# A batched A·Bᵀ on one Trainium2 core: one more batch of loads ahead of the first store, and a small early write into the output

## The chip, the cores and the metric

The kernel runs on one core of one Trainium2 chip. The metric is the device time of one execution, in microseconds (us). The kernel before took 126.73 us (median of 4; 126.66 to 126.77); over all the rounds in which it ran again beside the experiments, single runs of it went from 126.33 to 127.32, so one run alone says little about differences under 0.5 us.

## The reference

```python
def setup_inputs():
    batch, m, k, n = 16, 512, 512, 512
    return {"a": np.random.randn(batch, m, k).astype(np.float32),
            "b": np.random.randn(batch, n, k).astype(np.float32)}

def reference(a, b):
    return np.matmul(a, b.transpose(0, 2, 1)).astype(np.float32)
```

Sixteen independent products. Each batch reads 1 MB of a and 1 MB of b and writes 1 MB of out (1,048,576 bytes each): 48 transfers in all.

## The kernel before

Per batch it loads a and b, converts both to bf16 on VectorE, turns (transposes) them on TensorE, multiplies there, copies the result out of PSUM on ScalarE, and stores it. All 48 transfers are issued by SyncE, in program order:

```python
    AHEAD = 5
    apool = ctx.enter_context(tc.tile_pool(name="a_pool", bufs=6))
    bpool = ctx.enter_context(tc.tile_pool(name="b_pool", bufs=6))
    ...
    opool = ctx.enter_context(tc.tile_pool(name="o_pool", bufs=5))
    ...
    def load(i):
        a_sb = apool.tile([P, J, K], f32, tag="a")
        b_sb = bpool.tile([P, J, K], f32, tag="b")
        nc.sync.dma_start(a_sb[:], a[i].rearrange("(p j) k -> p j k", j=J))
        nc.sync.dma_start(b_sb[:], b[i].rearrange("(p j) k -> p j k", j=J))
        return a_sb, b_sb
    ...
    def store(i, o_sb):
        nc.sync.dma_start(out[i].rearrange("(p j) n -> p j n", j=J), o_sb[:])

    loaded = {}
    with tc.manual_schedule():
        for i in range(min(AHEAD, batch)):
            loaded[i] = load(i)
        for i in range(batch):
            a_sb, b_sb = loaded.pop(i)
            a_h = halve(a_sb, "a")                  # VectorE: f32 -> bf16
            b_h = halve(b_sb, "b")
            aT = turn(a_h, "a", nc.scalar.copy)     # TensorE, then a copy out of PSUM
            bT = turn(b_h, "b", nc.vector.tensor_copy)
            o_sb = multiply(aT, bT)                 # TensorE, then four ScalarE copies into o_sb
            store(i, o_sb)
            if i + AHEAD < batch:
                loaded[i + AHEAD] = load(i + AHEAD)
```

So ten loads precede store 0 in the queue; after that the order is store, load, load.

## Time and profile before

| What | Value | Where it is read |
|---|---|---|
| time, span | 126.73 us, 124.9 us | runs, page |
| TensorE, ScalarE, VectorE busy | 74%, 55%, 47% | page, part 1 |
| the SyncE queue's packets, as a share of 16 engines' span | 96.9% | page, part 3 |
| bytes over the span | 403 GB/s | page, part 3 |
| rate in the steady stretch, 40 to 80 us | 425 GB/s | stretches |
| rate from 25.5 to 28.0 us | 288 GB/s | stretches |

The transfer engines are the bound, so the way to read this profile is to look for places where they move less than 425 GB/s, and then to ask which of the sixteen ends last. A stretch in which they are busy (share near 1.00) and yet move clearly less is called a hole below; the turn is the place in the queue where the first store follows a run of loads. The trace keeps sixteen landing times for each transfer (768 for the 48), one for each engine's part; the transfer has landed at the last of them. The times don't carry the engine's name, so I sort them; an engine that lies a microsecond or more behind the other fifteen can still be followed from transfer to transfer. I use the landings below as a **lateness**: the landing time of an engine's part of transfer k, less 5.0 + 2.4526 x (k - 1) us. The slope is what the slowest engine of this kernel needed per transfer from transfer 13 to 48, (124.07 - 38.23)/35; the offset is arbitrary. A stall raises an engine's lateness, and it stays raised: in the kernel before the fastest engine stands at 0.91 us from transfer 10 and still at 0.95 at transfer 47. The line stands at 120.27 us for transfer 48, so a last landing 3.80 us late is one at 124.07.

### The profile page before, as it was taken

Reading aid. Unit: us, or ns where it says so; the run is one execution under the profiler, and the core shown is the slowest. Engines: PE = TensorE matmul, PEld = TensorE weight load, DVE = VectorE, ACT = ScalarE, POOL = GpSimd, SP = SyncE. Lnnn points to the kernel's source line nnn. Section 1 sums busy time; section 2 is a strip of 40 time slices with the busy share of each in tenths; the row PEclk is TensorE's granted clock in tenths of the full one; section 3 lists DMA queues with packets and bytes.
Section 4 is the critical chain, followed back from the end, with each engine's and each line's share of the span. In section 5 each row is a group of like instructions: output and inputs, shape, how many; then the busy total and the mean of one; then the engine's idle time right before and its main releaser. Section 6 shows DMA issues by size and latency. Waiting matters only on the chain.

```text
span 124.9 us, 1885 instructions
## 1 busy us (share of the span) xinstructions
PE 92.2 (74%) x754; PEld 55.9 (45%) x768; DVE 59.2 (47%) x64; ACT 68.3 (55%) x97; POOL 0.7 (1%) x6
## 2 busy tenths in 40 slices
PE   0069989898989878949586794958769495886900
PEld 0056465655656445534544453444445344454300
DVE  0156555647373554374446537444653645456000
ACT  4041576777767683755738275582826649173610
POOL 2000000000000000000000000000000000000000
PEclk9999999999999999999999999999999999999995
DMA  3999999999999999999999999999999999999982
GB/s 89 420 433 430 430 425 420 412 317 420 425 422 428 430 425 425 420 433 422 430 422 422 422 433 417 428 425 422 430 428 425 422 422 422 430 430 420 415 352 113
DMA packets 6922, 50.46 MB, mean 404 GB/s; under 512 B 769, under 2 KB 769, under 8 KB 769
## 3 DMA queue, kind: packets, MB, share of 16 engines
q1 hardware_dynamic: 6912, 50.33, 96.9%
q8 instruction: 6, 0.10, 0.3%
q14 instruction: 4, 0.02, 0.0%
HBM read 33.55 MB, written 16.78 MB: 403 GB/s over the span
## 4 chain that ended last, share of the span: by engine, by line
DMA 80%; DVE 6%; PE 5%; SPq 3%; issue 1%; ACT 0%; DVEq 0%
DMA b_sb<-in_b_dram 80%; DVE half L52 4%; PE ps L75 3%; PE tp L62 2%; DVE turned L67 2%; SPq L46 1%; SPq L47 1%; ACT o_sb L80 0%; DVEq L52 0%
## 5 line engine op out<-in xcount | busy, mean ns | idle before, releaser
L75 PE MATMUL ps<-turned 128*128 128x512 bf16 x242 | 59.8, 382 | 6.1 <-DVE turned L67 5.5
L80 ACT COPY o_sb<-ps 128x512 f32<-128x512 f32 x64 | 37.5, 586 | 44.0 <-PE ps L75 40.8
L62 PE MATMUL tp<-ident,half 128*128 128x128 bf16 x512 | 34.8, 225 | 20.1 <-DVE half L52 20.0
L62 PEld LDWEIGHTS <-half 128*128 128x128 bf16 x512 | 31.3, 101 | 25.6 <-DVE half L52 23.7
L75 PEld LDWEIGHTS <-turned 128*128 128x128 bf16 x256 | 25.1, 98 | 36.6 <-issue 10.7
L67 ACT COPY turned<-tp 128x1024 bf16<-128x1024 bf16 x32 | 30.8, 1016 | 6.0 <-PE tp L62 6.0
L52 DVE CAST half<-a_sb 128x2048 bf16<-128x2048 f32 x16 | 19.6, 1224 | 22.0 <-DMA a_sb<-in_a_dram 22.0
L67 DVE COPY turned<-tp 128x1024 bf16<-128x1024 bf16 x32 | 20.7, 686 | 19.3 <-PE tp L62 19.3
L52 DVE CAST half<-b_sb 128x2048 bf16<-128x2048 f32 x16 | 19.6, 1226 | 14.8 <-DMA b_sb<-in_b_dram 14.8
L67 ACT ACT_TABLE_LOAD x1 | 1.3, 1283 | 0.7 <-PEq L117 0.7
masks.py:199 POOL TENSOR_SCALAR_AFFINE_SELECT ident<-ident 128x128 bf16<-128x128 bf16 x1 | 0.3, 292 | 0.1
masks.py:197 POOL MEMSET ident<- 128x128 bf16 x1 | 0.2, 204 | 0.3 <-POOLq L117 0.3
L117 POOL MEMSET const-bfloat16-1.0<- 128x1 bf16 x1 | 0.1, 101 | 0.0
L117 POOL MEMSET const-uint8-127<- 128x1 uint8 x1 | 0.1, 101 | 0.0
L117 POOL MEMSET const-float32-0.0<- 128x1 f32 x1 | 0.1, 98 | 0.2 <-issue 0.2
L117 POOL MEMSET const-float32-1.0<- 128x1 f32 x1 | 0.1, 98 | 0.0
## 6 DMA issues: line engine op xcount, KB each, us to landing
a_sb<-in_a_dram SPq DMA_DIRECT2D x16, 1024.0 KB, 19.6
b_sb<-in_b_dram SPq DMA_DIRECT2D x16, 1024.0 KB, 19.6
out_dram<-o_sb SPq DMA_DIRECT2D x16, 1024.0 KB, 19.6
```

Source lines behind the costliest of these rows:

```text
L46: nc.sync.dma_start(a_sb[:], a[i].rearrange("(p j) k -> p j k", j=J))
L47: nc.sync.dma_start(b_sb[:], b[i].rearrange("(p j) k -> p j k", j=J))
L52: nc.vector.tensor_copy(out=half[:], in_=src[:])
L62: nc.tensor.transpose(tp[:, h, j * P:(j + 1) * P], half[:, j, (ko + h) * P:(ko + h + 1) * P], ident[:],)
L67: copy(out=turned[:, ko:ko + 2, :], in_=tp[:])
L75: nc.tensor.matmul(ps[:], aT[:, ko, j * P:(j + 1) * P], bT[:, ko, :], start=(ko == 0), stop=(ko == KO - 1),)
L80: nc.scalar.copy(out=o_sb[:, j, :].rearrange("m (p j) -> m p j", j=J), in_=ps[:].rearrange("m (j p) -> m p j", j=J),)
L117: nc = _bacc.Bacc("TRN2", target_bir_lowering=False, num_devices=1)
```

## The change

The intent, as far as the code tells it: the rate falls when the first store comes up, so a first write into out is made early, beside the start-up of the loads, and the first store is moved back by one batch. Two more load buffers are paid for by one output buffer.

```diff
-    AHEAD = 5
+    AHEAD = 6
-    apool = ctx.enter_context(tc.tile_pool(name="a_pool", bufs=6))
-    bpool = ctx.enter_context(tc.tile_pool(name="b_pool", bufs=6))
+    apool = ctx.enter_context(tc.tile_pool(name="a_pool", bufs=7))
+    bpool = ctx.enter_context(tc.tile_pool(name="b_pool", bufs=7))
-    opool = ctx.enter_context(tc.tile_pool(name="o_pool", bufs=5))
+    opool = ctx.enter_context(tc.tile_pool(name="o_pool", bufs=4))
...
+    zero = const.tile([P, P], f32)
+    nc.vector.memset(zero, 0.0)
     with tc.manual_schedule():
+        nc.scalar.dma_start(out[0].rearrange("(p j) n -> p j n", j=J)[:, 0, :P], zero[:])
         for i in range(min(AHEAD, batch)):
             loaded[i] = load(i)
```

## The prediction

> **What bounds the kernel now.** I read the page's rows of the span first, then stretches of the span, then the issue queue, then the end of the chain of waits. The page has the transfers near their ceiling in all but three places:
>
> ```profile
> DMA  3999999999999999999999999999999999999982
> GB/s 89 420 433 430 430 425 420 412 317 420 425 422 428 430 425 425 420 433 422 430 422 422 422 433 417 428 425 422 430 428 425 422 422 422 430 430 420 415 352 113
> HBM read 33.55 MB, written 16.78 MB: 403 GB/s over the span
> ```
>
> A slice is 124.9/40 = 3.12 us. No engine is above 74% (PE) over the span, so compute only matters where a transfer waits for it. The weak slices are the first (89, start-up), the ninth (317, at 25.0 to 28.1 us) and the last two (352, 113). The stretches, cut at the edges of these holes (columns: stretch, length, busy time and count on PE, weight loads, VectorE, ScalarE, GpSimd, then clock, DMA share, GB/s):
>
> ```profile
> 3.12:24.50 21.38, 16.12 (x130) 10.64 (x133) 11.27 (x13) 10.29 (x14) 0.00 (x0) 1.00 1.01 424
> 25.50:28.00 2.50, 2.50 (x23) 1.49 (x21) 0.99 (x1) 1.68 (x4) 0.00 (x0) 1.00 1.00 288
> 40.00:80.00 40.00, 31.45 (x264) 18.80 (x267) 20.00 (x22) 23.31 (x34) 0.00 (x0) 1.00 1.01 425
> 118.40:120.10 1.70, 0.06 (x1) 0.00 (x0) 0.00 (x0) 0.58 (x1) 0.00 (x0) 1.00 0.70 294
> ```
>
> From 25.5 to 28.0 us the DMA share stays 1.00 while the rate falls to 288: the engines have work, but it goes slowly. The loss is 2.50 x (1 - 288/425) = 0.81 us averaged over the sixteen engines. It is the only such place in mid-run. Ten loads of 1 MB precede store 0 in the one SyncE queue; the tenth is moving then, and store 0 is next. All later stores pass at 425. So something is paid once, around the first turn from loads to stores.
>
> The issue queue shows it from the side of the slowest engine (start, duration):
>
> ```profile
> 5.64 0.33 SPq L46 DMA_DIRECT2D a_sb<-in_a_dram  x1
> 8.08 0.33 SPq L47 DMA_DIRECT2D b_sb<-in_b_dram  x1
> 16.30 0.35 SPq L87 DMA_DIRECT2D out_dram<-o_sb  x1
> ...
> 24.54 0.33 SPq L47 DMA_DIRECT2D b_sb<-in_b_dram  x1
> 28.10 0.34 SPq L87 DMA_DIRECT2D out_dram<-o_sb  x1
> 30.91 0.33 SPq L46 DMA_DIRECT2D a_sb<-in_a_dram  x1
> 33.37 0.33 SPq L47 DMA_DIRECT2D b_sb<-in_b_dram  x1
> ```
>
> The trace has eight semaphores for transfers, so a transfer is issued when the one eight before it has landed on its slowest engine. The issues at 5.64, 24.54 and 30.91 therefore time the landings of transfers 1, 8 and 10. In the steady part issues are (92.33 - 53.04)/16 = 2.456 us apart: the time of 1 MB. From 5.64, seven more should end at 22.83; the eighth ends at 24.5, 1.65 late. From there two more should end at 29.4; the tenth ends at 30.9, 1.5 late. The landings' records agree: the first of the sixteen engines finishes transfer 8 at 22.49 and the last at 24.48, and an instruction fetch of 16 KB sits at 22.1 (1.0 us) on one engine. That engine stays some 2.4 to 2.8 us behind the fastest to the end.
>
> Budget: 5.64 + 47 x 2.456 = 121.07; the last landing is at 124.07; the 3.0 between are the fetch and restart on the slow engine (about 1.6) and the first-store hole (about 1.45 on that engine, 0.8 on average). The span ends 0.8 later, and the time is 1.8 over the span.
>
> The end of the chain (start, us, what):
>
> ```profile
> 92.33 19.57 DMA b_sb<-in_b_dram
> 111.90 0.03 issue
> ...
> 118.49 0.58 ACT o_sb L80
> ```
>
> The last load lands at 111.90, its result is ready at 119.07, the last store goes out at 119.1. The page ends its chain in compute, but this is not what binds: fast engines drain at about 118.4 and idle (the 294 above), while the slow engine lands store 14 at 121.65 and store 15 at 124.07, 2.42 later, which is one transfer without a pause. The end belongs to the slow engine's unbroken stream.
>
> **What the Trainium skill says.** "HBM Reference", Specifications: a core streaming alone reaches about 425 GB/s, bounded by its 16 engines. The trace agrees: 424 and 425. "DMA: Bandwidth & Descriptors", Issuing engines are not separate DMA queues: what ScalarE issues runs on the same sixteen engines and interleaves. So the zeros bring no bandwidth. No second issuing queue is in this trace, but the instruction fetches, a foreign queue too, do displace packets: at 71.37 an 8 KB fetch took 0.31 us and the packet after it 0.86 instead of 0.31. The same page, Back-pressure in remote DMA: stalled writes stall an engine's other queues too. That is said for remote transfers; nothing in this trace shows whether it holds for a first write to out. It is the main argument against the change.
>
> **The change part by part.**
>
> *AHEAD 5 to 6, pools of 7.* Two loads change places with store 0: it becomes transfer 13 of 48 and starts some 4.9 us later. No bytes are added. Store 0's data is ready at 16.3; as transfer 13 it would get its semaphore when transfer 5 lands, at 15.5, so SyncE is not blocked longer than now, and eight transfers (19.6 us of work) stay queued. The hole would merely move from 26 to about 31 us. At the end the last load is transfer 42 in place of 43, so compute of batch 15 gets 2.456 us more lead. This end doesn't bind, so it is worth 0.
>
> *o_pool 5 to 4.* In steady state store i is transfer 13+3i, and load b of batch i+4 is transfer 3i+9. The first eviction of batch i+4 comes 115.90 - 111.90 = 4.0 us after that landing, but now needs store i, four transfers later, 9.8 us. So ScalarE will wait some 5.8 us for each buffer: a new wait. It paces compute at one batch per three transfers (7.37 us), against some 5.9 that a batch needs (first evictions at 24.90, 30.80, 36.70), so it holds the rhythm and starves no transfer: a store is due 12 transfers after the one whose buffer it took. In the tail, batch 14 evicts when store 10 lands (transfer 43), four evictions of 0.58 back to back are 2.4, the two turned copies of batch 15 are 1.93, its first eviction comes some 0.6 later and its last ends 3.2 after that: 8.1 us after the landing of transfer 43. Transfer 47 lands 9.8 after it, and a store needs about 1 us from issue to its first packet. Slack is 0.7 against 1.5 now: thin, worth 0.
>
> *The zeros.* One memset of 128x128 on VectorE (GpSimd's of that form took 0.20 us) and one issue on ScalarE (0.4 as SyncE's first ones), both before ScalarE's first copy at 8.00: off the path. On the engines 64 KB are 8 pieces of 512 B each, 4 KB in all: 0.15 us of bytes at 26.6 GB/s an engine. If they fall into the first 1.1 us, in which the first load packets wait for their data, they cost about 0.2; in a running stream about 0.15 + 0.55 for the restart, as after the fetch: 0.7. I take 0.4, an estimate. Store 0 must wait for the zeros to land, long past by then.
>
> If the hole is the price of the first write to out, and if it is paid beside the start-up, the slow engine gains 1.4: 126.73 - 1.4 + 0.4 = 125.7.
>
> **Rivals.**
> 1. *The stall moves and isn't hidden.* The zeros pay it at 2 to 5 us and block the loads of the same engine: 126.73 + 0.4 = 127.1. For: the shared engines and the back-pressure above. Against: the engines do nothing useful there for the first microsecond anyway (slice one has 89 GB/s).
> 2. *The hole isn't the first write.* The slow packets are those of the tenth load (3rd to 8th of its 8 on most engines, 0.4 to 0.64 us instead of 0.31), and store 0's own run at 0.31. It could be tied to the turn from loads to stores or to something else in time. Then the hole stays, at 26 or at 31 us: again 127.1. Against: it ends exactly as store 0 begins, and no later turn has it.
> 3. *The o_pool's wait becomes the bound in the tail.* If ScalarE's chain is 1 us longer than I worked out, the last store leaves late by some 0.3, and all engines end late: up to 0.5 more.
> 4. *The order of fetches changes*, and the hole and the 16 KB fetch no longer strike one engine twice: up to 0.5 less, down to 125.2.
>
> **Range and chances.** I give the hidden stall 0.6 and rivals 1 and 2 together 0.4: 0.6 x 125.7 + 0.4 x 127.1 = 126.3; rival 4 is likelier than rival 3, so I say 126.1. The range 125.2 to 127.3 takes in both outcomes. 2% would be 2.5 us; the whole of the hole and half of the fetch would have to go to be faster by that, and a wait that nothing here shows would have to come to be slower by it: 0.03, 0.94, 0.03.
>
> **What will show it.** Right, if: no slice after the first falls under 400 GB/s before the tail; issues on SyncE are 2.46 apart through the first store; the last landing is some 1 us earlier; the first load lands at 5.6 to 6.1; ScalarE's evictions name the store as what they waited for, with no hole in GB/s. Wrong, if: the hole appears at 31 us (rival 2); the first loads land a microsecond later than 5.64 (rival 1); the last store is issued less than 1 us before the slow engine is through with transfer 47 (rival 3).

## The result, and the profile after

The changed kernel took 126.85 us (median of 4; 126.72 to 126.95) against 126.73 (126.66 to 126.77). The ratio is 1.0009, with a 95% interval of 0.9992 to 1.0027: no difference. The measured time lies inside the predicted range and its class (within 2%) is the one forecast, but the gain of 0.6 us that the prediction called for did not come. It was wrong.

The rows of the page after, over 40 slices of 3.13 us:

```profile
DMA  3999999999999999999999999999999999999964
GB/s 65 419 427 429 435 424 419 411 424 421 380 427 411 424 424 421 429 424 421 429 419 424 432 424 419 419 429 437 424 427 411 429 429 429 424 421 419 416 270 175
```

The hole of the ninth slice (317) is gone. The eleventh, where store 0 now comes up, has 380: the hole moved and is shallower. The first slice lost (65, it was 89), and the loss in the tail is deeper (270 for 352). The stretches of the kernel after, cut at its own hole (columns as in the prediction: stretch, length, busy time and count of five engines, clock, DMA share, GB/s):

```profile
3.12:30.50 27.38, 21.68 (x178) 13.91 (x178) 14.35 (x16) 14.48 (x20) 0.00 (x0) 1.00 1.01 423
30.50:33.00 2.50, 2.49 (x13) 1.16 (x12) 2.46 (x3) 1.17 (x2) 0.00 (x0) 1.00 0.99 380
40.00:80.00 40.00, 32.53 (x275) 19.04 (x273) 20.70 (x23) 21.84 (x34) 0.00 (x0) 0.96 1.01 425
```

380 where it was 288. By averages the change did what it was meant to do. The issue queue tells what the slowest engine saw (start, duration; a transfer is issued when the one eight before it has landed on its slowest engine):

```profile
5.88 0.33 SPq L47 DMA_DIRECT2D b_sb<-in_b_dram  x1
8.40 0.33 SPq L47 DMA_DIRECT2D b_sb<-in_b_dram  x1
...
20.83 0.33 SPq L47 DMA_DIRECT2D b_sb<-in_b_dram  x1
24.85 0.34 SPq L87 DMA_DIRECT2D out_dram<-o_sb  x1
27.35 0.33 SPq L46 DMA_DIRECT2D a_sb<-in_a_dram  x1
...
32.33 0.34 SPq L87 DMA_DIRECT2D out_dram<-o_sb  x1
36.00 0.33 SPq L46 DMA_DIRECT2D a_sb<-in_a_dram  x1
38.46 0.33 SPq L47 DMA_DIRECT2D b_sb<-in_b_dram  x1
```

The first landing shows at 5.88 for 5.64 before, the second at 8.40 for 8.08: the start lost 0.24 and then 0.32 us. From 20.83 to 24.85 is the instruction fetch (a packet of 16 KB that the queue of kind "instruction" moved at 22.43 over one engine; it took 1.02 us), 4.02 for a transfer of 2.46, as before. And from 32.33 to 36.00 a transfer takes 3.67: the slowest engine still loses 1.2 us where store 0 comes up. Its stream then runs on at 2.45 to the last landing at 124.25, 3.98 late.

The zeros themselves did not move in the first microsecond, where the prediction put their cost at 0.2 us. ScalarE issued them at 1.03 us, but their 128 packets are in the trace from 5.14 to 5.56 us, behind the first load and in a stream that was already running (from 4.5 to 6.2 us, q10 is ScalarE's queue):

```profile
1.03 0.41 ACTq L95 DMA_DIRECT2D out_dram<-zero  x1
```

```profile
q1 hardware_dynamic: 96, 0.66, 91.5%
q10 hardware_dynamic: 144, 0.07, 13.2%
```

Nearly all of the first load's data had moved by then, so most of its 0.24 us was lost before a single zero moved.

Mean and slowest lateness, from the landings:

| | before | after |
|---|---|---|
| mean, transfer 2 | 0.43 | 0.80 |
| mean, two transfers before store 0 and two after it | 0.75, 1.51 | 1.19, 1.70 |
| slowest engine, the same two | 2.34, 3.80 | 2.74, 4.07 |
| fastest and slowest engine, transfer 48 | 2.52, 3.80 | 3.56, 3.98 |

So the mean loss at the first store fell from 0.77 to 0.51 us (in the second there is a further instruction fetch, some 1.5 us on one engine, 0.09 of the mean). The slowest engine's loss fell from 1.46 to 1.33. Against that stands about 0.37 us at the start on average, and on the slowest engine 0.40 when it comes to the turn (2.74 for 2.34).

ScalarE's waits show the new wait that the smaller o_pool brings (who waited for whom: total, times, longest):

```profile
ACT o_sb L80 <- DMA out_dram<-o_sb: 36.9, 11, 3.5
```

No such line exists before. It holds up no transfer. The last step of the after's chain ends at 120.13 (first row: start and length of the last copy; second: when SyncE began and ended the run of six last issues):

```profile
119.55 0.58 ACT o_sb L80
```

```profile
92.49 28.00 SPq L87 DMA_DIRECT2D out_dram<-o_sb  x6
```

Store 15 goes out at 120.15. The slowest engine lands store 14 at 121.81, so it had 1.66 us in hand (2.55 before, 121.65 less 119.10). The fifteen other engines ended store 15 between 123.83 and 124.01 (the fastest of them stood 1.17 late at transfer 47 and 3.56 at 48, so it had run dry and waited for the issue); the slowest ended at 124.25. The output ring's wait came within 0.25 us of becoming the bound.

### The profile page after: what moved, and what is told of

Read it like the earlier page. It is cut to its first block, busy times and chain, and to the rows that moved or that the text cites. A ratio compares the mean times of both kernels' runs of the same rounds, so it can differ in the third digit from the quotient of the medians.

```text
span 125.2 us, 1900 instructions
## 1 busy us (share of the span) xinstructions
PE 95.4 (76%) x768; PEld 55.9 (45%) x768; DVE 58.7 (47%) x65; ACT 65.1 (52%) x97; POOL 0.7 (1%) x6
## 4 chain that ended last, share of the span: by engine, by line
DMA 83%; PE 8%; ACT 3%; issue 1%; DVE 1%; SPq 0%; ACTq 0%
DMA out_dram<-o_sb 32%; DMA b_sb<-in_b_dram 31%; DMA a_sb<-in_a_dram 20%; PE ps L75 7%; ACT o_sb L80 2%; ACT turned L67 1%; PE tp L62 1%; DVE turned L67 1%; SPq L87 0%; ACTq L80 0%; SPq L46 0%; SPq L47 0%
## 5 line engine op out<-in xcount | busy, mean ns | idle before, releaser
L75 PE MATMUL ps<-turned 128*128 128x512 bf16 x256 | 64.9, 400 | 16.3 <-ACT turned L67 13.9
L80 ACT COPY o_sb<-ps 128x512 f32<-128x512 f32 x64 | 34.3, 595 | 48.1 <-DMA out_dram<-o_sb 36.9
L62 PE MATMUL tp<-ident,half 128*128 128x128 bf16 x512 | 33.0, 225 | 7.8 <-DVE half L52 7.8
L67 ACT COPY turned<-tp 128x1024 bf16<-128x1024 bf16 x32 | 31.3, 1044 | 5.5 <-PE tp L62 5.5
```

The lines of the kernel that those rows point to most:

```text
L62: nc.tensor.transpose(tp[:, h, j * P:(j + 1) * P], half[:, j, (ko + h) * P:(ko + h + 1) * P], ident[:],)
L67: copy(out=turned[:, ko:ko + 2, :], in_=tp[:])
L75: nc.tensor.matmul(ps[:], aT[:, ko, j * P:(j + 1) * P], bT[:, ko, :], start=(ko == 0), stop=(ko == KO - 1),)
L80: nc.scalar.copy(out=o_sb[:, j, :].rearrange("m (p j) -> m p j", j=J), in_=ps[:].rearrange("m (j p) -> m p j", j=J),)
```

## The experiments

Eighteen runs: variants of one trace each, and three repeats. Averages quoted as "mean loss" are the rise of the mean lateness from transfer 9 to 13 (11 to 15 where AHEAD is 6), that is around store 0. Several runs compute nothing ("transfers only"): they are there to see the queue by itself. Their outputs are wrong, which doesn't matter for the times.

### 1. The order and the pools without the zeros, and the zeros without them

e1_order_only is the changed kernel less three lines, e2_zeros_only is the kernel before plus them:

```diff
-    zero = const.tile([P, P], f32)
-    nc.vector.memset(zero, 0.0)
-        nc.scalar.dma_start(out[0].rearrange("(p j) n -> p j n", j=J)[:, 0, :P], zero[:])
```

> The change without the zeros: AHEAD 6, pools of 7, 7 and 4. Theory (the zeros removed most of the first-store hole on fifteen engines and cost 0.3 us at the start; order and pools are worth nothing): the hole of 0.8 us on average is back, on all engines, at about 31 us in place of 26; the first load lands at 5.6 as before; time within 0.2 us of before (126.7). Rival (the later first store alone shrank the hole): no slice near 31 us falls under 390 GB/s, time about 126.5.

Measured: 126.87 us against 126.91, ratio 1.0009 (0.9982 to 1.0035). The hole is at 31 us, on all engines:

```profile
30.50:33.00 2.50, 2.50 (x17) 1.20 (x15) 1.47 (x2) 1.67 (x4) 0.00 (x0) 1.00 0.94 351
```

Mean loss 0.59; the first load lands as before. The slowest engine goes from 2.21 to 3.86. The order and the pools are worth nothing in time, as predicted. The hole has 351 GB/s for 288 at 26 us, as many as with the zeros alone (next run). So the shallower hole of the changed kernel can't be put down to the zeros alone; its two traces have mean losses of 0.51 and 0.30, against 0.59 here.

> The kernel before with the zeros alone: AHEAD 5, pools of 6, 6 and 5. Theory: first load lands 0.3 us later, the hole at 26 us shrinks on the median engine from 0.9 to about 0.25 us, but the slowest engine keeps one packet of 1.4 to 1.8 us there; time 126.7 to 126.9. Rival (the zeros do nothing, the changed order did): the hole of 0.8 us at 26 us stays, time about 127.0.

Measured: 126.88 us against 126.91, ratio 0.9995 (0.9983 to 1.0007). From 25.5 to 28.0 us the rate is 351 in place of 288:

```profile
25.50:28.00 2.50, 2.50 (x13) 1.16 (x12) 2.03 (x2) 1.50 (x3) 0.00 (x0) 1.00 0.99 351
```

Mean loss 0.38 for 0.77. The slowest engine goes from 2.62 to 3.63, a loss of 1.01 for 1.46, but it was 0.28 later when it got there. That leaves it 0.17 ahead after the turn, and small losses later took this back: the last landing is 3.79 late, before had 3.80.

### 2. Transfers only, without and with the zeros

The compute between load and store is cut and every store reads one tile of ones:

```diff
-            a_h = halve(a_sb, "a")
...
-            store(i, o_sb)
+            store(i, o_all)
```

> Wrong on purpose: the 48 transfers of before in the same order, stores from a tile of ones, no compute, so TensorE fetches no instructions. Theory (the slowest engine is the one that the fetch at 22 us delayed by 1.5 us, and it also pays its own hole): no engine is late before the first store, landings stay within 0.6 us of each other until 25 us, the hole of some 0.9 us on all engines remains, and the time falls to about 124.0 (126.7 less 1.5 for the fetch, less some 0.6 by which the slowest engine paid more, less up to 0.5 in the tail). Rival (one engine has a packet of 1.5 us or more at the first store whatever its lag): one landing of the sixteen is again 1 us or more behind the others after the first store, time about 125.

Measured: 125.66 us (ratio 0.9902, 0.9882 to 0.9922). No engine is late before the first store: all sixteen landings of transfer 9 lie within 0.4 us. The hole is there:

```profile
25.50:28.00 2.50, 0.00 (x0) 0.00 (x0) 1.00 1.01 321
```

The mean loss is 0.75, the slowest engine goes from 0.87 to 2.33. The trace has no packet of 16 KB. The hole therefore needs no compute and no instruction fetch, and the largest loss doesn't need a late engine: one engine, at most 0.87 late before the turn, lost at least 1.45 us there, as much as the late one of the kernel before. The time fell by 1.25 us, not by the 2.7 that I had expected: engines fell behind in small steps later on, and the last landing is 2.98 late for 3.80.

> Wrong on purpose: the same transfers with the zeros before them. Theory: the start is 0.3 us later, the hole shrinks to under 0.3 us on the median engine; if no engine keeps a long packet, time 0.4 to 0.6 us under the kernel of transfers alone. Rival (one engine always keeps a packet of about 1.5 us at the first store, zeros or not): time 0 to 0.3 us above the kernel of transfers alone.

Measured: 125.77 us, ratio to before 0.9914 (0.9897 to 0.993), no different from the run without zeros. 347 GB/s in the hole, mean loss 0.51, and the mean lateness of transfer 2 is 0.70 for 0.41. After the turn (transfer 13) the mean lateness is 1.44, without zeros 1.39: gain and cost cancel here too.

### 3. What do the zeros do? Size, target, place, queue

```diff
 e5_small_zeros (on the kernel before):
-    ...j=J)[:, 0, :P], zero[:])
+    ...j=J)[:16, 0, :P], zero[:16, :])
 e6_sbuf_zeros (transfers only):
-        nc.scalar.dma_start(out[0].rearrange(...)[:, 0, :P], zero[:])
+        nc.scalar.dma_start(zero2[:], zero[:])
 e7_zeros_last (transfers only):
-        nc.scalar.dma_start(out[0].rearrange(...)[:, 0, :P], zero[:])
+        nc.scalar.dma_start(out[batch - 1].rearrange(...)[:, 0, :P], zero[:])
 e12_zeros_sync (transfers only): the zeros go on SyncE, between the first a and the first b
```

> The kernel before with the zeros of 16 rows of 512 bytes, one piece for each of the sixteen engines in place of eight. So far the zeros took some 0.35 us off every engine's loss at the first store and put 0.35 us on its start. Theory (what is paid once is an engine's first write to out, whatever its size): the loss from transfer 9 to 13 falls from 0.76 us on average to about 0.4, the start is under 0.15 us late, the slowest engine's last landing is some 0.2 us earlier, time 126.5. Rival (the cost at the start is a cost of the bytes and pieces, and the relief at the first store goes with it): the loss at the first store is 0.65 or more, time as before within 0.1 us.

Measured: 126.87 us against 126.98, ratio 0.9999 (0.9975 to 1.0023). Each engine has now written 512 bytes into out before store 0, the start is no later (mean of transfer 2: 0.45), and the hole is there in full:

```profile
25.50:28.00 2.50, 2.50 (x25) 1.57 (x23) 0.81 (x1) 1.86 (x4) 0.00 (x0) 1.00 0.88 285
```

Mean loss 0.78, the slowest engine from 2.34 to 4.22. An engine's first write into out, as such, is not what is paid for.

> Wrong on purpose: transfers only, and ScalarE's small transfer goes from SBUF to SBUF, so nothing is written to out before store 0. Theory (the first write to HBM counts): the mean loss from transfer 9 to 13 is about 0.75 us as with no zeros (0.75), time 0.2 to 0.4 us over that of the kernel of transfers alone. Rival (the first read of SBUF by a transfer counts, or only the disturbance by a second queue): the loss is about 0.5 us as with zeros into out (0.51).

Measured: 125.83 us. Nothing is written to out before store 0, and the hole is shallower than in any run of this order:

```profile
25.50:28.00 2.50, 0.00 (x0) 0.00 (x0) 1.00 0.99 377
```

Mean loss 0.25, mean of transfer 2 at 0.77. The expectation from "the first write to HBM counts" was 0.75. That theory falls: 64 KB within SBUF relieve the turn at least as much as 64 KB into out.

> Wrong on purpose: transfers only, the zeros go into the last batch of out, 15 MB away from store 0. Theory (a first write to out at any place counts): mean loss from transfer 9 to 13 about 0.5 us. Rival (the place counts, store 0 needs its own addresses touched): about 0.75 us, and a smaller one at store 15.

Measured: 125.94 us, 364 GB/s in the hole, mean loss 0.34, transfer 2 at 0.70. Up to transfer 13 the place does not matter, as would follow from e6, and there is no smaller hole at store 15. But the loss then comes after all: the mean lateness is 1.27 at transfer 13 and 1.69 at transfer 15. Measured from transfer 9 to 16, the mean loss is 0.80 here, 0.58, 0.38 and 0.63 in the other runs with the 64 KB (e4, e6, e12), and 0.77 and 0.83 with transfers alone (e3 and its repeat). So the relief can be a delay; why it was one in this trace I don't know.

> Wrong on purpose: transfers only, the zeros into out go as the second transfer of SyncE's own queue. Theory (a second queue on the engines isn't needed, the small pieces are): lateness after transfer 2 about 0.35 us more than without zeros, mean loss from transfer 9 to 13 about 0.3 to 0.5. Rival (the second queue made the difference): lateness 0.25 to 0.35 us more after the zeros, loss 0.75.

Measured: 125.92 us, 360 GB/s, mean loss 0.43. The queue does not matter either, which agrees with what the prediction quotes of the Trainium skill ("DMA: Bandwidth & Descriptors", Issuing engines are not separate DMA queues). The relief comes with 128 pieces of 512 bytes moved near the start, whoever issues them and wherever they go, and it goes with their cost.

### 4. Is it only a later start?

```diff
+        if i == 0:
+            nc.vector.memset(a_sb[:, 0, :320], 0.0)
         nc.sync.dma_start(a_sb[:], a[i].rearrange("(p j) k -> p j k", j=J))
```

> Wrong on purpose: transfers only, no zeros; the first load waits for a memset of VectorE and starts some 0.4 us later. Theory (zeros or a copy within SBUF relieve the first store by something that their pieces do to the engines' queues): mean loss from transfer 9 to 13 stays at 0.75 us, time 0.3 to 0.5 us over that of transfers alone. Rival (a later start alone is won back at the first store): loss about 0.3 to 0.5 us and time within 0.2 us of it.

Measured: 125.80 us. The mean lateness of transfer 2 is 0.92 (0.5 later than with transfers alone), the rate in the hole 328 GB/s, the mean loss 0.57. That is between the two: some of it may be won back by a late start alone, but less than with the pieces. Its last landing is 3.07 late, with transfers alone 2.98 and 2.97: of the 0.5 us at the start, 0.1 is left at the end, partly won back at the turn and partly later. So how much of the relief is due to the pieces and how much to the later start that comes with them is not separated by these runs.

### 5. Where does the hole belong?

```diff
-    AHEAD = 5
+    AHEAD = 1
```

> Wrong on purpose: transfers only, without zeros, in the order load, load, store from the start, so store 0 is the third transfer and not the eleventh. Theory (a price of the first turn from loads to stores, paid wherever it comes): a mean loss of 0.7 to 0.8 us between transfers 2 and 6, slowest engine's last landing about as with transfers alone (123.3), time 125.5 to 125.8. Rival (the hole comes from ten loads in front, or from a point in time): no loss over 0.3 us near 8 us; if of time, one at 26 us; without any, time about 124.9.

Measured: 126.18 us. The price is paid where the first store is: the mean lateness goes from 0.31 at transfer 1 to 1.93 at transfer 4, more than the 0.7 to 0.8 expected (from 7 to 8 us the engines' share fell to 0.64, so in part the engines stood idle). There is no hole at 26 us: 426 GB/s. So it's neither a point in time nor the ten loads in front.

```diff
-        for i in range(min(AHEAD, batch)):
-            loaded[i] = load(i)
...
+        for s in range(3):
+            for i in range(5 * s, 5 * s + 5):
+                load(i)
+            store(s, o_all)
+        load(15)
+        for i in range(3, batch):
+            store(i, o_all)
```

> Wrong on purpose: transfers only, in the order ten loads, store 0, ten loads, store 1, ten loads, store 2, two loads, thirteen stores. Theory (a price of the first turn alone): mean lateness rises by 0.6 to 0.8 us around store 0 (transfer 11) and by under 0.2 around store 1 (22) and store 2 (33). Rival (a price of every store after a long run of loads): it rises by 0.5 us or more each time, so the last landing is a microsecond or more later than with transfers alone.

Measured: 125.67 us. At store 0 the mean rises from 0.64 (transfer 9) to 1.38 (transfer 12); at store 1 from 1.65 (21) to 1.71 (23); at store 2 not at all. The stretches around the three stores:

```profile
25.50:28.00 2.50, 0.00 (x0) 0.00 (x0) 1.00 0.87 288
52.00:57.00 5.00, 0.00 (x0) 0.00 (x0) 1.00 1.01 423
80.00:85.00 5.00, 0.00 (x0) 0.00 (x0) 1.00 1.00 421
```

It is a price of the first turn from loads to stores. A later store after just as long a run of loads does not pay it.

### 6. Why is the slowest engine so slow?

In the kernel the slowest engine is 1.5 us behind from the fetch when the turn comes, and loses more there than the others. Coincidence, or does an engine that is late lose more?

```diff
+    lag = const.tile([1, 17, K], f32)
     with tc.manual_schedule():
+        nc.scalar.dma_start(lag[:], a[0, :17, :].rearrange("(o r) k -> o r k", o=1))
```

> Wrong on purpose: transfers only, with a further load of 34 KB into one partition at the start, which should fall on one engine alone and make it some 1.3 us late. Theory (a late engine loses more at the turn): it is 1.3 to 1.5 us behind before transfer 10 and loses 1.3 to 1.7 us there, against 0.6 to 0.8 on average; it ends last, later than with transfers alone. Rival: it loses what the others lose, 0.3 to 1.0 us.

Measured: 126.25 us (2 runs). The 17 rows of 2 KB went to one engine. The landings of three transfers, all sixteen engines, as lateness in us:

```
transfer  9:  0.46 0.46 0.48 0.54 0.61 0.62 0.62 0.63 0.67 0.67 0.71 0.72 0.72 0.74 0.75 | 1.96   mean 0.71
transfer 10:  0.86 0.92 0.93 0.94 0.97 1.00 1.00 1.40 1.46 1.48 1.48 1.56 1.57 1.57 1.58 | 3.77   mean 1.41
transfer 13:  0.89 0.94 0.98 1.00 1.01 1.05 1.06 1.53 1.54 1.61 1.62 1.74 1.76 2.00 2.05 | 3.68   mean 1.53
```

There are three kinds of engine: about half lose 0.4 us, the other half 0.8 or more, and the one that came late by 1.2 us loses 1.7. It ends 3.71 late, where the last of the transfers alone ended 2.98. In this trace, and in all seven of a full kernel with store 0 after ten or twelve loads, the engine that came late was among the hardest hit, at 1.01 to 1.88 us against means of 0.30 to 0.82. That lateness is the cause is likely and not shown: with transfers alone, where no engine was more than 0.90 late, one still lost at least 1.45 (e3) and 1.39 (its repeat), and this is one trace. What is shown is why the average misled me: the loss that bounds the kernel isn't the average one, and it adds to what the engine was already behind.

### 7. Repeats

> The kernel before once more, for a second trace: how far do the measures repeat from run to run? Expected if they are good for differences of 0.2 us: mean loss from transfer 9 to 13 again 0.7 to 0.8 us, slowest engine's loss there 1.3 to 1.6, last landing 124.0 to 124.2 us, time 126.7 to 126.9. If they aren't, these differ by 0.3 us or more and the smaller differences found so far mean nothing.

Measured: 126.74 us (2 runs). Mean loss 0.62 (0.77 in the first trace), slowest engine from 1.99 to 3.66, last landing 3.88 late, 318 GB/s in the hole. Single traces repeat to about 0.2 us in the mean loss and on the slowest engine.

> The changed kernel once more, for a second trace. First load 0.25 us and second load 0.35 us later than before, mean loss from transfer 11 to 15 about 0.4 to 0.5 us (0.6 to 0.8 before), slowest engine's loss there 1.2 to 1.4, last landing 124.1 to 124.3, time 126.7 to 127.0.

Measured: 126.75 us (2 runs). Transfer 2 at 0.78, mean loss 0.30, 406 GB/s in the hole, slowest engine from 2.81 to 3.95, last landing 3.87 late. The hole was smaller still than in the first trace, and the time was the same.

> Wrong on purpose: the transfers alone once more, for a second trace. Mean loss from transfer 9 to 13 about 0.75 us if the first trace was typical; if it is 0.5 or less, the relief that zeros or a copy within SBUF seemed to give there isn't shown by single traces.

Measured: 125.94 us (2 runs). Mean loss 0.81, 298 GB/s: the hole of transfers alone repeats. Over all runs with ten loads in front, those without the 64 KB have 285, 288, 288, 295, 298, 318 and 321 GB/s from 25.5 to 28.0 us (328 with the late start), those with it 347, 351, 360, 364 and 377. In this window the relief is real; that it lasts is shown less well (e7).

### 8. Using it: the turn before the fetch

If a late engine loses more, the turn should come while no engine is late, that is before the fetch at 22 us.

```diff
 e10_store_third: six loads before store 0, loads 3 to 5 after it
-        for i in range(min(AHEAD, batch)):
+        for i in range(3):
 e17_store_at_seven: the a of batch 3 as well before store 0, its b after it
+        a3 = load_a(3)
 e18_store_at_eight: four whole batches before store 0
+        for i in range(4):
```

> Store 0 is queued after six loads in place of ten; all else of the kernel before is unchanged. The turn to stores then comes at about 18 us, before the fetch at 22 us. Theory (the slowest engine is slowest because it is already 1.5 us behind the others when they turn, and then loses 1.45 in place of 0.76): it loses no more than the others at the turn, the last landing is 0.4 to 0.7 us earlier, time 126.0 to 126.4. Rival (the loss at the turn falls on an engine whatever its lag): slowest engine again 3.6 us or more late, time 126.6 to 127.0; worse, if store 0 reaches the queue after it has drained at 17.7 us.

Measured: 127.63 us, ratio 1.0091 (1.0057 to 1.0125): slower by 0.9%, clear of the noise. Store 0 was issued at 16.56. From 17 to 18 us the engines' share fell to 0.82, so some stood idle; from 18.5 to 21.0 they were busy (1.00) and moved 249 GB/s. Transfer 9 has a mean lateness of 1.78, for 0.75 before. The run says nothing of the theory, as the turn and a queue with little in it came together: SyncE's issues, one after the other, took up to 1.03 us each there.

> Kernel before, with store 0 queued after seven transfers (three batches and the a of the fourth) in place of ten; the order from store 1 on is that of before. The queue holds work until 20.2 us when store 0 is issued at 16.5, so it doesn't drain. Theory (late engines lose more at the turn; here no engine is late yet): the slow packets come at 18 to 20.5 us, the slowest engine loses 0.9 to 1.3 us there, the fetch at about 22 us then costs one engine 1.5, last landing 3.0 to 3.5 us behind the line in place of 3.8, time 126.1 to 126.5. Rival (what is saved at the turn comes back at the next stores or elsewhere): last landing again 3.6 to 4.0 behind, time 126.6 to 127.0.

Measured: 126.91 us against 126.83, ratio 1.0009 (0.9988 to 1.003). The turn did come early, and the slowest engine lost 0.97 there (0.82 late at transfer 6, 1.79 at transfer 7). Two stretches, at store 0 and where the next loss fell:

```profile
18.50:21.00 2.50, 2.50 (x13) 1.12 (x12) 1.74 (x2) 1.76 (x3) 0.00 (x0) 1.00 0.91 311
24.80:26.80 2.00, 2.00 (x11) 0.94 (x10) 0.20 (x1) 1.44 (x3) 0.00 (x0) 1.00 1.04 393
```

But by transfer 9 several have lost again, in packets of 0.87 to 1.41 us at 25.1 us, with the fetch at 22.8 in between; the slowest is at 3.30 and ends 3.89 late. What was saved at the turn came back.

> The same with store 0 after eight transfers (four batches): the slow packets come at 20.5 to 23 us and overlap the fetch. Theory: between the two, last landing 3.2 to 3.8 us behind the line, time 126.3 to 126.7. Rival: as before, 126.6 to 127.0.

Measured: 126.8 us against 126.83, ratio 1.0004 (0.9989 to 1.0018). Slowest engine 2.65 late at transfer 9 and 2.82 until transfer 19, a microsecond better than before. Then later fetches struck engines of the slower half, and five engines end at 3.68 to 3.81. The same end by another way.

No version here beats the kernel before.

## Why the prediction was wrong

**What held.** The bound (the slowest engine's unbroken stream) is right: in both kernels it decides the last landing. The order and the load pools are worth 0 (e1: ratio 1.0009). The zeros' cost, taken as 0.4 us, was 0.3 to 0.4 on average and 0.5 on the slowest engine (below). Of the signs that the prediction named, the hole came at 31 us (rival 2); the first load was 0.24 us late and not a microsecond (rival 1), and the last store was issued 1.66 us before the slow engine was ready for it (rival 3). The prediction put the wait for an output buffer at some 5.8 us; it was up to 3.5 us, and it starved nothing, as said. The slack in the tail, counted after the 1 us from issue to first packet (the first load: issued at 0.73, first packet at 1.75), was put at 0.7 and is 0.66 (1.66 - 1.0). One reading was a little off: the slow engine stays 2.7 to 3.0 us behind the fastest, not 2.4 to 2.8.

**The step that failed** is this one: "If the hole is the price of the first write to out, and if it is paid beside the start-up, the slow engine gains 1.4". Neither if held.

- It is not the price of the first write to out. With one small write by every engine the hole stayed in full (e5, mean loss 0.78); with 64 KB that never touch out it shrank to 0.25 (e6). It is paid at the first turn from loads to stores, wherever that comes (e8), and not at the second (e13). Rival 2 of the prediction, "tied to the turn from loads to stores", was the right one. It got less than its due because the hole "ends exactly as store 0 begins", which fits both.
- It was not paid beside the start-up either: the zeros moved at 5.14 to 5.56 us, in a running stream, and what relief there is is not free. On the slowest engine the 64 KB cut the loss at the turn from 1.46, 1.67, 1.88 and 1.65 us (before, its repeat, e5, e1; mean 1.67) to 1.33, 1.14 and 1.01 (after, its repeat, e2; mean 1.16). That is 0.5 us, not 1.4. And they made the start some 0.35 us later; when the slowest engine came to the turn, it was 2.34, 1.99, 2.34 and 2.21 us late without (mean 2.22) and 2.74, 2.81 and 2.62 with (mean 2.72), 0.5 us more. After the turn the slowest engine stands at 3.80, 3.66, 4.22 and 3.86 us without (mean 3.88) and at 4.07, 3.95 and 3.63 with (mean 3.88).

The sum in the prediction's own form is then 126.73 - 0.5 + 0.5, so 126.7 as an estimate from these numbers, and the measured 126.85 is within the scatter of the runs (those of before, beside later experiments, went from 126.33 to 127.32).

**What the average hid.** I had worked out 0.81 us for the average and 1.45 for the slowest engine, and took both to have one cause that one remedy would remove in full. The slowest engine's place has a second cause: the fetch puts it 1.2 us or more behind the others before the turn, and its loss there, about twice the mean, comes on top (e14, an engine made late on purpose: 1.72 against 0.82; whether being late is why it loses more is not shown, see e3). The change made the average hole shallower, 380 and 406 GB/s for 288, and the bound didn't follow.

**Rival 4** (the fetch and the hole no longer strike one engine) did not happen in the changed kernel: the fetch at 22.4 us still precedes the turn. Where I forced it (e17, e18), the gain was lost by later stalls.

**What stays open.** I don't know what in the hardware is paid at the first turn, nor why a few hundred nanoseconds of small pieces near the start relieve it by about as much as they cost, nor how much of that is only the later start (e11) or a delay of the loss (e7). Nor is it shown why the last landing comes out at 3.8 to 4.0 us late in nearly every variant of the full kernel, by quite different ways. The Trainium skill's "DMA: Bandwidth & Descriptors", Back-pressure in remote DMA, was quoted in the prediction as the main argument against the change; no run here shows or refutes stalled writes as the mechanism.

## What to carry to other kernels

When the transfer engines are the bound, don't read a hole in GB/s as time to be won: follow the engine that lands last, because its loss can have another size than the average, and the average can improve with no gain at all. A one-off stall at a first event tempts one to "warm up" that event; try the warm-up with a target that can't matter (here a copy within SBUF) before believing in it, and count what it costs at the start. Moving the stall is not removing it: three ways of moving the first store gave 126.8 to 126.9 us, and a fourth, with store 0 after only six loads, gave 127.6.

## What the Trainium skill lacked or had wrong

- "DMA: Bandwidth & Descriptors" says nothing of a loss at the first turn of a queue from loads to stores: 285 to 321 GB/s for 2.5 us in place of 425, a mean loss of 0.6 to 0.8 us, and from at least 1.2 (e13) to 1.88 us (e5) on the engine that loses most.
- No page that I found gives the price of an instruction fetch to the transfers of the DMA engine that it runs on (it would belong to "Runtime: NRT & Kernel Launch"): here 16 KB took 1.02 us, and the packet after it 0.86 in place of 0.31, so that one engine lost about 1.5 us.
- "DMA: Bandwidth & Descriptors", Specifications, gives 512 bytes as the least for line rate. Here the pieces of 512 bytes took 27 ns each (all 128 of the kernel after), 19 bytes per ns on an engine; those of 8,192 took 309 ns (median), 26.5 bytes per ns. Seven tenths of the rate, then.
